# A layer with 32 experts on one core: half of a small projection moved from the middle of the kernel into the first gather, and the low halves of the last token block moved to GpSimd

## The chip, the core and the metric

The kernel runs on one core of a Trainium2 chip. Its engines work side by side and wait for one another by semaphores: TensorE (PE in the profile, PEld for its weight loads) multiplies, VectorE (DVE) and ScalarE (ACT) do elementwise work, GpSimd (POOL) does some of it more slowly, and SyncE (SP) issues all transfers, one after the other, from a queue of its own. The metric is the device time of one execution in microseconds (us); lower is better.

## The reference

One layer over 512 tokens of width 1024, in float32. Cut to what matters here:

```python
x = x + mixed @ w_out                         # attention and recurrence, merged
t = rmsnorm(x, g_moe)
fine = t @ w_rt_expert + b_rt_expert          # routing: top group, then two of its experts
top_logit, top_idx = lax.top_k(fine_sel, 2)
hid = silu(t @ wg) * (t @ wu)                 # 32 experts, 1024 -> 512 -> 1024
acc = acc + c[:, None] * (hid @ wd)
...
gate = sigmoid(rmsnorm(x, g_ple) @ w_ple_gate)
x = x + gate * (p @ w_ple_proj)               # p is 512 x 256, w_ple_proj 256 x 1024
```

p @ w_ple_proj depends on inputs alone. It may be computed anywhere, and is needed only in the last step.

## The kernel before

It works in this order: norm and transposes of x; the recurrent branch; its output projection (`r_stage(0)` to `r_stage(3)`); attention by pairs of heads; its output projection; the product with `w_out` (`out_mm`) with the routing of each block of 128 tokens; the experts, two at a time (`experts(pr)`, 16 pairs); the gate and the final norm.

Accurate products are made of three fast ones: each operand is split into a high part (a copy on ACT into the type fp32r) and a low part (the difference, on VectorE or GpSimd), and high x high, high x low and low x high are added in PSUM (`wsplit` for weights, where a counter hands every third low part to GpSimd).

**p's projection.** `turn_p` transposes and splits p, `p_proj(i)` multiplies it with 512 columns of `w_ple_proj` (24 products for four token blocks), copies the result to SBUF and writes it to the DRAM tile `pp_dram`, which the last stage reads back. `p_proj(0)` stands between `r_stage(1)` and `r_stage(2)`, `p_proj(1)` between `r_stage(2)` and `r_stage(3)`.

**Routing and first gather.** For token block t, `out_route` makes the last logits, `route` picks group and experts (a chain of some 20 small operations on VectorE), ranks the tokens of each expert by products with 0/1 matrices (`rk`), and `one_hot` writes a selection matrix. `split_tokens(t)` makes the high and low half of the block's normed rows (`HX[t]`). `gather_mm` multiplies rows by selection: 16 products for each block, 64 in all, accumulate the tokens of the first four experts (`pt0`, copied to `xg`). For blocks 0 to 2 these stand behind the routing of block 3 in the program; a scheduler may draw them ahead of it. Block 3's follow when its selection is there. Then the first pair's products start: `pair_front`, 16 steps (8 with "g" weights, 8 with "u" weights).

**The ring.** Expert weights come as tiles of 1 MiB, 12 for a pair, 192 in all, into a ring of 15 places (`ra0` to `ra10`, `rb0` to `rb3`) in that order of use, and two more (the first two u tiles of pair 0) into the pool `once`. So 17 tiles can be loaded ahead of the first expert. Every further load waits until the product that reads the tile in its place is done. Four places (`rb0` to `rb3`) hold the merged branches until `out_mm` has read them. Low tiles of memory (`mo`, `once`) share addresses with pools of the earlier stages and come free when those are done. After step 12 of pair 0 the kernel closes `once` and makes the combine weights and their rows (`late_routing`, `in_rows`, on TensorE `row_ps`).

`in_order` fixes TensorE's order for the experts; elsewhere a scheduler orders ready work by priority, and the queues of all engines are fixed before the run. A count `nblk` decides a branch (never taken here) that all engines pass before the experts' main part.

Of the kernel before, what the change touches and what calls it, by code (L numbers as in the profile page):

```python
# [40 lines left out]
def kernel(  # L41
# [20 lines left out]
    def in_order(eng=mybir.EngineType.PE):  # L62
# [6 lines left out]
        for i in ins[start:]:  # L69
            if i.engine == eng:  # L70
# [1 line left out]
                    tc.add_manual_dep(i, prev.name, mybir.DependencyInfo(mybir.DependencyClass.NoSync,  # L72
                                                                         mybir.DependencyReason.DATA), reason="in_order")
                prev = i
    RING_A, RING_B = 11, 4
    W_EARLY = 1
    NRING = RING_A + RING_B
    ONCE = 2

    def SM(name, shape, dt=F32, bufs=4):  # L80
# [459 lines left out]


    pp_dram = dram.tile([S, D], F32, name="pp_dram")

    def turn_p():

        pt = sps("pT_ps")
        for k in range(2):
            for t in range(NT):
                nc.tensor.transpose(pt[:, k, t * P:(t + 1) * P],
                                    pl[t // 2][:, t % 2 * PLE + k * P:t % 2 * PLE + (k + 1) * P], ident)  # L550
            hi, lo = (klp.tile([P, S], F32R, tag=f"kl{n}{k}", bufs=1, name="pt") for n in range(2))
            nc.scalar.activation(hi, pt[:, k, :], AF.Copy)
            nc.vector.tensor_sub(lo, pt[:, k, :], f32(hi))
            PT.append((hi, lo))

    def p_proj(i):
        wh, wl = wsplit(wpp[:, :, i * 512:(i + 1) * 512], [P, 2, 512])
        for t in range(NT):
            ts = slice(t * P, (t + 1) * P)
            if t % 2 == 0:  # L560
                pz2 = sps("pp_ps")
            pz = pz2[:, t % 2, :]
            for k in range(2):
                nc.tensor.matmul(pz, PT[k][0][:, ts], wh[:, k, :], start=k == 0, stop=False)
                nc.tensor.matmul(pz, PT[k][0][:, ts], wl[:, k, :], start=False, stop=False)
                nc.tensor.matmul(pz, PT[k][1][:, ts], wh[:, k, :], start=False, stop=k == 1)
            pe = T("pp")
            nc.scalar.activation(pe, pz, AF.Copy)
            nc.sync.dma_start(pp_dram[ts, i * 512:(i + 1) * 512], pe)

    PT = []
    r_stage(0)
    turn_p()
    r_stage(1)
    wpp = WR([P, 2, D])
    nc.sync.dma_start(wpp, w_ple_proj[0].rearrange("(k p) c -> p k c", p=P))
    p_proj(0)
    r_stage(2)
    p_proj(1)
    r_stage(3)  # L580
    KL = [[klp.tile([P, S], F32R, tag=f"kl{j}{c}", bufs=1, name=f"kl{j}{c}") for c in range(2)] for j in range(2)]
    for j in range(2):
# [85 lines left out]

    G, E = L[:, :, 0:4], L[:, :, 4:36]

    def route(t):

        t0, t1, n, ts_, hs = t, t + 1, 1, (t,), slice(t, t + 1)
        first_max(G, rev4, v4, gmx, f4, t0, t1)
        for t in ts_:
            nc.vector.tensor_scalar(pen[:, t], v4[:, t], f4[:, t:t + 1], NEG, op0=ALU.is_lt, op1=ALU.mult)
        Eh = E[:, hs].rearrange("p t (g e) -> p t g e", g=4)
        nc.vector.tensor_tensor(Eh, Eh, pen[:, hs, :, None].to_broadcast([P, n, 4, 8]), op=ALU.add)
        first_max(E, rev32, v32, m1, f1, t0, t1)
        for t in ts_:  # L680
            nc.vector.tensor_scalar(oh[:, 0, t], v32[:, t], f1[:, t:t + 1], None, op0=ALU.is_equal)
        nc.vector.scalar_tensor_tensor(E[:, hs], oh[:, 0, hs], NEG, E[:, hs], op0=ALU.mult, op1=ALU.add)
        first_max(E, rev32, v32, m2, f2, t0, t1)
        for t in ts_:
            nc.vector.tensor_scalar(oh[:, 1, t], v32[:, t], f2[:, t:t + 1], None, op0=ALU.is_equal)
        rk = tps("rk_ps")[:, 0, 0:32]
        nc.tensor.matmul(rk, ones[0:1, :], e1024b, start=True, stop=False)
        for t2 in range(t):
            for i in range(2):
                nc.tensor.matmul(rk, ones, oh[:, i, t2, :], start=False, stop=False)  # L690
        for i in range(2):
            nc.tensor.matmul(rk, upper, oh[:, i, t, :], start=False, stop=i == 1)
        for i in range(2):
            nc.vector.scalar_tensor_tensor(ohr[:, i, t], oh[:, i, t], 1.0, rk, op0=ALU.mult, op1=ALU.mult,
                                           accum_out=pos[:, i, t:t + 1])

    def split_tokens(t, hx):

        HX[t] = hx
        for i in range(2):  # L700
            cs = slice(i * 512, (i + 1) * 512)
            nc.scalar.activation(hx[:, 0, cs], xm[:, t, cs], AF.Copy, scale=rstd2[:, t:t + 1])
            nc.vector.scalar_tensor_tensor(hx[:, 1, cs], xm[:, t, cs], rstd2[:, t:t + 1], f32(hx[:, 0, cs]),
                                           op0=ALU.mult, op1=ALU.subtract)

# [3 lines left out]
    def one_hot(oneh, pq, t):  # L709
        nc.vector.tensor_scalar(oneh[:, t, :], iota, pq[:, 0, t:t + 1], None, op0=ALU.is_equal)  # L710
        return nc.vector.scalar_tensor_tensor(oneh[:, t, :], iota, pq[:, 1, t:t + 1], f32(oneh[:, t, :]),  # L711
                                       op0=ALU.is_equal, op1=ALU.add)

    def gather_mm(oneh, o, k, ts_):

        for t in ts_:
            for i in range(2):
                c0 = k // 2 * 256 + k % 2
                nc.tensor.matmul(o, HX[t][:, i, c0:c0 + 255:2], oneh[:, t, :],  # L719
                                 start=t == 0 and i == 0 and k % 2 == 0, stop=t == NT - 1 and i == 1 and k % 2 == 1)  # L720

    oneh0 = ONEH()
    pt0 = [sps("xg0_ps").rearrange("p a (k s) -> p (a k) s", k=2) for _ in range(2)]
# [35 lines left out]
        with tc.high_priority():  # L759
            turned[0] = nc.scalar.activation(xTs[j, tt], pt[:, 0:2, :], AF.Copy)  # L760

    def out_route(j, tt):
        for k in range(2):
            kk = 2 * j + k
            nc.tensor.matmul(lg[j, tt], xTs[j, tt][:, k, :], rw[:, kk, :], start=k == 0, stop=k == 1)
        with tc.high_priority():
# [11 lines left out]
        route(tt)  # L778
        hot[0] = one_hot(oneh0, pos, tt)
    wo = {}  # L780
    prev = None
    for j, tt in [(j, t) for j in range(2) for t in range(NT)] + [(j, t) for t in range(NT) for j in (2, 3)]:
        if j not in wo:
            raw = wraw(w_out[0], 256 * j)
            wo[j] = wo_block(raw, 0, False) + wo_block(raw, 1, 3 == j)
        pz = zps("out_ps")[:, 0:256]
        out_mm(pz, wo[j], tt, range(2))
        if prev:
            out_turn(*prev)
        out_mm(pz, wo[j], tt, range(2, KT))  # L790
        if prev:
            out_route(*prev)
        out_add(j, tt, pz)
        prev = j, tt
    with tc.high_priority():
        out_turn(*prev)
        out_route(*prev)
    for k in range(KT):
        gather_mm(oneh0, pt0[k // 4][:, k % 4, :], k, range(3))


    mx_stack.close()
# [4 lines left out]
    ring = [(ring_a, f"ra{i}") for i in range(RING_A)] + [(ring_b, f"rb{i}") for i in range(RING_B)]  # L807

    def RING(name, dt=F32):

# [4 lines left out]
    W = {}  # L815

    def gate_load(b):
        W["ple", b] = WR([P, 2, D]) if b < 3 else mo.tile([P, 2, D], F32, tag="hx3", bufs=1, name="wgr")
        nc.sync.dma_start(W["ple", b], w_ple_gate[0, 256 * b:256 * b + 256, :].rearrange("(k p) c -> p k c", p=P))

    def pair_order():
# [5 lines left out]
                yield pr - 1, "d", w_e_down  # L827
        yield NE // 2 - 1, "d", w_e_down

    def loads():  # L830
        for pr, nm, src in pair_order():
            if pr == 15 and nm == "d":
                for b in range(W_EARLY):
                    gate_load(b)
            for h in range(4):
                n = P if nm == "d" else 2 * P
                if (pr, nm) == (0, "u") and h < ONCE:
                    t = once.tile([P, 2, D], F32, name=f"once{h}")
                else:
                    t = RING(nm)  # L840
                s_ = src[0, 2 * pr:2 * pr + 2, h * n:(h + 1) * n, :]
                s_ = s_.rearrange("e (p k) f -> p e (k f)", k=2)
# [3 lines left out]
                nc.sync.dma_start(*W[pr, nm, h])  # L846
                yield

    loader = loads()
# [9 lines left out]
        used[0] += n  # L859
        load_upto(used[0] + (ONCE if used[0] < 8 else 0) + len(ring))  # L860

    load_upto(NRING + ONCE - 0)

    late = []

    def MT(name, shape=(P, 512), dt=F32):
        return late[0].tile(list(shape), dt, tag="mt", bufs=6, name=name)

    split_tokens(3, mo.tile([P, 2, D], F32R, tag="hx3", bufs=1, name="hx3"))
    posb = mo.tile([P, 2, S], F32, name="posb")  # L870
    wb = mo.tile([P, 2, S], F32, name="wb")
    pcol = mo.tile([P, NE // 2], F32, name="pcol")
# [247 lines left out]
    def front_fill(pr):  # L1120
        def fill(step, last):
# [3 lines left out]
                scatter_two(pr - 2, 0)  # L1125
            if step == SLOTS_AT and pr:
                slots_of(pr - 1)
            if pr == 0 and step == 12:
                once_stack.close()
                late.append(ctx.enter_context(tc.tile_pool(name="late", bufs=1)))  # L1130
                with tc.issue_after(last.ins):
                    late_routing()
                    in_rows(pos, posb)
                    in_rows(wts, wb)
# [172 lines left out]
```

## Time and profile before

| | |
|---|---|
| time, median of 3 runs | 1128.45 us (1127.37 to 1129.65) |
| the profiled execution | 1131.39 us, its span 1129.7 us |
| TensorE busy | 1096.9 us, 97% of the span |
| VectorE, ScalarE, GpSimd busy | 568.0, 382.6, 156.1 us |
| mean granted TensorE clock | 0.987 of full speed |

A row of the timeline gives the start, the length, the engine, the line of the kernel, what is written and read, the shape, a count, and in brackets how long the engine sat idle before it and for whom. Products follow each other faster than the length of one, since they are pipelined: the distance of their starts is their cost. Line numbers are those of the kernel before. Names drop their buffer numbers: `wr` is a weight buffer or, in the gather, a block's rows, `hx` the rows of block 3.

### The profile page before, as it was taken

The page shows a single profiled execution, that of the slowest core. Times are in us where ns is not written, and L with a number is a line of the kernel's source. Part 1 is how long each engine was busy: PE and PEld are TensorE (multiplying, and loading weights), DVE is VectorE, ACT ScalarE, POOL GpSimd, SP SyncE. Part 2 cuts the span into 40 slices and gives each one's busy share as a digit, 9 for nine tenths or more (in the row PEclk, how much of TensorE's full clock was granted, in tenths as well). Part 3 has the DMA queues.
Part 4 walks back from the last instruction along what each step waited for, and adds up shares of the span by engine and source line. Part 5 has one row for each costly group of instructions (what it writes and reads, how often), then busy time and mean ns, then how long its engine had stood idle before and what let it go on. Part 6 is the DMA issues. An engine that isn't in the chain of part 4 may idle for free. (4 is left out here: it accounts for less than half of the span.)

```text
span 1129.7 us, 14413 instructions
## 1 busy us (share of the span) xinstructions
PE 1096.9 (97%) x5650; PEld 740.1 (66%) x5650; DVE 568.0 (50%) x1080; ACT 382.6 (34%) x771; POOL 156.1 (14%) x142
## 2 busy tenths in 40 slices
PE   8999999999999999999989999999999999999897
PEld 7777777788787878778984535353545353533376
DVE  5766675236566574664474334334333334233653
ACT  5455544335455454634322202020202011111443
POOL 4242423111122121233100000000000000000201
PEclk8999999999999999999999999999999999999899
DMA  7322231522222212136748999999999999999601
GB/s 207 112 87 82 74 132 60 184 84 72 72 75 75 76 62 75 52 108 233 270 176 307 396 413 413 412 414 413 412 412 411 412 413 414 413 413 416 270 20 56
DMA packets 101602, 259.81 MB, mean 230 GB/s; under 512 B 12477, under 2 KB 56090, under 8 KB 93338
## 3 DMA queue, kind: packets, MB, share of 16 engines
q1 hardware_dynamic: 101530, 258.84, 60.2%
q8 instruction: 46, 0.75, 0.3%
q14 instruction: 26, 0.21, 0.1%
HBM read 254.63 MB, written 4.19 MB: 229 GB/s over the span
## 5 line engine op out<-in xcount | busy, mean ns | idle before, releaser
L1032 PE MATMUL y_ps<-d,hT 128*64 128x512 f32 x512 | 118.3, 602 | 2.2 <-DMA d<-in_w_e_down_dram 2.2
L158 ACT ACTIVATE wh<-wr 128x1024 fp32r<-128x1024 f32 x81 | 85.5, 1057 | 98.1 <-PE R_ps L171 21.9
L1018 PE MATMUL gu_ps<-g,xg 128*64 128x512 f32 x512 | 116.8, 595 | 0.1
L1018 PE MATMUL gu_ps<-u,xg 128*64 128x512 f32 x496 | 110.1, 592 | 0.0
L161 DVE TENSOR_TENSOR wl<-wr,wh 128x1024 fp32r<-128x1024 f32 x54 | 73.0, 1352 | 60.3 <-ACT wh L158 58.9
L161 POOL TENSOR_TENSOR wl<-wr,wh 128x1024 fp32r<-128x1024 f32 x27 | 66.0, 2444 | 175.3 <-ACT wh L158 161.9
L1023 ACT ACTIVATE sg<-gu_ps 128x512 f32<-128x512 f32 x16 | 9.6, 598 | 235.5 <-PE gu_ps L1018 235.5
L1032 PEld LDWEIGHTS y_ps<-d,hT 128*64 128x64 f32 x512 | 36.2, 138 | 73.2 <-issue 67.2
L1018 PEld LDWEIGHTS gu_ps<-g,xg 128*64 128x64 f32 x512 | 37.1, 137 | 69.1 <-issue 64.4
L1018 PEld LDWEIGHTS gu_ps<-u,xg 128*64 128x64 f32 x496 | 35.8, 137 | 70.3 <-issue 69.0
L1024 DVE TENSOR_TENSOR sg<-sg,gu_ps 128x512 f32<-128x512 f32 x16 | 11.0, 687 | 120.8 <-ACT sg L1023 120.8
L1223 POOL TENSOR_TENSOR wgl<-wr,wgh 128x1024 fp32r<-128x1024 f32 x2 | 4.7, 2380 | 481.1 <-DMA PP<-pp_dram 481.1
L994 DVE TENSOR_TENSOR xm<-xm,comb_ps 128x1024 f32<-128x1024 f32 x30 | 36.6, 1221 | 60.5 <-PE comb_ps L993 60.5
L719 PE MATMUL xg_ps<-oneh,wr 128*128 128x256 f32 x384 | 58.2, 290 | 2.1 <-DVE oneh L711 2.1
L976 DVE SCALAR_TENSOR_TENSOR yl<-y_ps,c,yh 128x512 fp32r<-128x512 f32 x30 | 22.5, 750 | 73.4 <-ACT yh L975 71.5
L975 ACT ACTIVATE yh<-y_ps,c 128x512 fp32r<-128x512 f32 x30 | 20.6, 688 | 100.6 <-PE y_ps L1032 100.6
L719 PEld LDWEIGHTS xg_ps<-oneh,wr 128*128 128x128 f32 x384 | 52.7, 201 | 2.8 <-DVE oneh L711 2.2
L172 PE MATMUL merge_ps<-hTh,wl 128*128 128x512 f32 x128 | 51.8, 405 | 0.0
L170 PE MATMUL merge_ps<-hTh,wh 128*128 128x512 f32 x128 | 51.4, 402 | 0.0
L171 PE MATMUL merge_ps<-hTl,wh 128*128 128x512 f32 x128 | 51.4, 401 | 0.0
L985 DVE TENSOR_TENSOR xm<-xm,comb_ps 128x512 f32<-128x512 f32 x68 | 43.8, 680 | 4.7 <-PE comb_ps L983 4.4
L944 ACT ACTIVATE xg<-xg_ps,gm 128x256 f32<-128x256 f32 x60 | 25.2, 471 | 53.6 <-PE xg_ps L719 53.5
(329 smaller groups left out, 2526.4 us busy)
## 6 DMA issues: line engine op xcount, KB each, us to landing
g<-in_w_e_gate_dram SPq DMA_DIRECT2D x64, 1024.0 KB, 18.9
d<-in_w_e_down_dram SPq DMA_DIRECT2D x64, 1024.0 KB, 19.9
u<-in_w_e_up_dram SPq DMA_DIRECT2D x62, 1024.0 KB, 18.7
wr<-in_w_in_dram SPq DMA_DIRECT2D x26, 1024.0 KB, 5.1
wr<-in_w_lru_br_dram SPq DMA_DIRECT2D x4, 1024.0 KB
wr<-in_w_attn_br_dram SPq DMA_DIRECT2D x4, 1024.0 KB, 5.2
wr<-in_w_out_dram SPq DMA_DIRECT2D x4, 1024.0 KB, 5.2
wr<-in_w_ple_gate_dram SPq DMA_DIRECT2D x3, 1024.0 KB
```

The lines of the kernel that those rows point to most:

```text
L158: nc.scalar.activation(hi, src, AF.Copy)
L161: e.tensor_sub(lo, src, f32(hi))
L170: nc.tensor.matmul(out_ps, wh[:, k, :], th(k), start=k == 0, stop=False)
L171: nc.tensor.matmul(out_ps, wh[:, k, :], tl(k), start=False, stop=False)
L172: last = nc.tensor.matmul(out_ps, wl[:, k, :], th(k), start=False, stop=k == KT - 1)
L719: nc.tensor.matmul(o, HX[t][:, i, c0:c0 + 255:2], oneh[:, t, :], start=t == 0 and i == 0 and k % 2 == 0, stop=t == NT - 1 and i == 1 and k ...
L944: xg_out["a"] = nc.scalar.activation(xg[(k + c) // 2][:, (k + c) % 2, :], pt[:, c, :], AF.Copy, scale=gm2[:, k + c:k + c + 1])
L976: nc.vector.scalar_tensor_tensor(yl, y, c[:, 0:1], f32(yh), op0=ALU.mult, op1=ALU.subtract)
L985: nc.vector.tensor_tensor(xs_, xs_, pc, op=ALU.add)
L994: nc.vector.tensor_tensor(xm[:, t, :], xm[:, t, :], pc.rearrange("p a b -> p (a b)"), op=ALU.add)
L1018: last = nc.tensor.matmul(gu[i][64 * e:64 * e + 64, :], xg[k // 2][:, k % 2, o + 64 * e:o + 64 * e + 64], W[pr, nm, k // 2][0][:, e, k % 2 ...
L1032: nc.tensor.matmul(py[i][64 * e:64 * e + 64, :], hT[:, f, 64 * e:64 * e + 64], W[pr, "d", f // 2 * 2 + e][0][:, f % 2, i * 512:(i + 1) * 5 ...
```

## The change

The second half of p's projection leaves its place between `r_stage(2)` and `r_stage(3)`. `turn_p` now also writes the transposed p to DRAM (`pt_dram`); before the last part of `out_mm` is built, `p_split` reads it and the second half of `w_ple_proj` back in four loads of 256 KB and splits them on ACT and VectorE. The 24 products (`p_late(0)` to `p_late(3)`, six for each token block) stand in the first gather, in an order written out by hand. Block 3's low halves are made on GpSimd, from an extra copy on ACT; its rows get a place of the ring's memory (`hx3`), and the ring's fifteenth place moves to `mo` (`rc`). The tiles in `once` are now the last two u tiles of pair 0, and they are issued behind all others. `once` is closed after step 15.

```diff
-    RING_A, RING_B = 11, 4
+    RING_A, RING_B = 10, 4
-    NRING = RING_A + RING_B
+    NRING = RING_A + RING_B + 1
...
 def turn_p():
+            raw = T("praw")
+            nc.scalar.activation(raw, pt[:, k, :], AF.Copy)
+            nc.sync.dma_start(pt_dram[k], raw)
...
     r_stage(2)
-    p_proj(1)
     r_stage(3)
...
 def split_tokens(t, hx):
             nc.scalar.activation(hx[:, 0, cs], xm[:, t, cs], AF.Copy, scale=rstd2[:, t:t + 1])
+            if t == 3:
+                xn = PE("xn")
+                nc.scalar.activation(xn, xm[:, t, cs], AF.Copy, scale=rstd2[:, t:t + 1])
+                nc.gpsimd.tensor_sub(hx[:, 1, cs], xn, f32(hx[:, 0, cs]))
+                continue
...
+    def p_late(t):
+        pz = zps("pp2_ps")
+        p_mm(pz, t, lambda k: wp2[k][0], lambda k: wp2[k][1])
+        p_keep(pz, t, 1, PE("pe"))
+    PE = lambda name: mr.tile([P, S], F32, tag="pe", bufs=3, name=name)
+    def p_split():
+        for (hi, lo), src in zip(wp2 + PT, (wpp2[:, 0, 512:1024], wpp2[:, 1, 512:1024], pt_dram[0], pt_dram[1])):
+            raw = PE("p2raw")
+            nc.sync.dma_start(raw, src)
+            nc.scalar.activation(hi, raw, AF.Copy)
+            nc.vector.tensor_sub(lo, raw, f32(hi))
...
-    with tc.high_priority():
-        out_turn(*prev)
-        out_route(*prev)
-    for k in range(KT):
-        gather_mm(oneh0, pt0[k // 4][:, k % 4, :], k, range(3))
+    def fill():
+        p_late(0)
+        gather0(2)
+    with in_order():
+        gather0(0)
+        with tc.high_priority():
+            out_turn(*prev)
+        gather0(1)
+        with tc.high_priority():
+            out_route(*prev, fill, lambda: p_late(1))
+        p_late(2)
+        p_late(3)
...
-                if (pr, nm) == (0, "u") and h < ONCE:
+                if (pr, nm) == (0, "u") and h >= 4 - ONCE:
...
-    load_upto(NRING + ONCE - 0)
+    load_upto(NRING + ONCE)
+    for z in later:
+        nc.sync.dma_start(*z)
-    split_tokens(3, mo.tile([P, 2, D], F32R, tag="hx3", bufs=1, name="hx3"))
...
-            if pr == 0 and step == 12:
+            if pr == 0 and step == 15:
```

TensorE's queue at the end of the first gather, before: the last products of blocks 0 to 2 (`xg_ps<-oneh,wr`) stand between the rank and count products (`rk_ps`, `cnt_ps`), then block 3's 16, then three steps of the first pair, and the branch.

```order
L719 MATMUL xg_ps<-oneh,wr 128x256 x8
L884 LDWEIGHTS ones
L884 MATMUL cnt_ps<-oh,ones 128x32
L692 LDWEIGHTS upper
L692 MATMUL rk_ps<-oh,upper 128x32
L719 MATMUL xg_ps<-oneh,wr 128x256 x8
L719 MATMUL xg_ps<-oneh,hx_5231 128x256 x16
L1018 MATMUL gu_ps<-g,xg 64x512 x3
```

After, from the second half of block 0's gather on (`xmT_ps<-ident,xm` is the last transpose before the logits `xmT_ps<-rw,xmT` of block 3; `pp_ps<-p` are p's products):

```order
L742 MATMUL xg_ps<-oneh,wr 128x256 x9
L792 MATMUL xmT_ps<-ident,xm 128x128 x2
L742 MATMUL xg_ps<-oneh,wr 128x256 x16
L800 MATMUL xmT_ps<-rw,xmT 128x36 x2
L563 MATMUL pp_ps<-p_4368,p_4372 128x512
L564 MATMUL pp_ps<-p_4369,p_4372 128x512
L565 MATMUL pp_ps<-p_4368,p_4373 128x512
L563 MATMUL pp_ps<-p_4370,p_4374 128x512
L564 MATMUL pp_ps<-p_4371,p_4374 128x512
L565 MATMUL pp_ps<-p_4370,p_4375 128x512
L742 MATMUL xg_ps<-oneh,wr 128x256 x16
L563 MATMUL pp_ps<-p_4368,p_4372 128x512
```

Six products of p now stand ahead of block 2's gather and six behind it, ahead of the rank products; twelve more stand between the rank products and block 3's gather. The transpose and the logits of block 3 each stand behind a whole block's gather.

SyncE's queue ahead of the branch, before (g, u, d are ring loads):

```order
L846 DMA g<-in_w_e_gate_dram 128x2x1024 x4
L846 DMA u<-in_w_e_up_dram 128x2x1024 x4
L846 DMA d<-in_w_e_down_dram 128x2048
L846 DMA once_5205<-in_w_e_up_dram 128x2x1024
L846 DMA once_5207<-in_w_e_up_dram 128x2x1024
L1158 TENSOR_LOAD nblk_i
L1158 ISA x2
L1159 COMPARE_AND_BRANCH
```

And after:

```order
L900 DMA u<-in_w_e_up_dram 128x2x1024 x4
L569 DMA pp_dram<-pe 128x512 x3
L900 DMA d<-in_w_e_down_dram 128x2048
L569 DMA pp_dram<-pe 128x512
L1213 TENSOR_LOAD nblk_i
L1213 ISA x2
L900 DMA d<-in_w_e_down_dram 128x2048
L918 DMA once_5247<-in_w_e_up_dram 128x2x1024
L918 DMA once_5248<-in_w_e_up_dram 128x2x1024
L900 DMA d<-in_w_e_down_dram 128x2048
L1214 COMPARE_AND_BRANCH
```

The first d load (into `rc`) now stands behind three of the four writes of p's results. The second d load, which waits until the first expert's products have read a g tile, stands ahead of the two `once` loads, which before were issued ahead of all experts.

## Rows read from the trace of the kernel before

**Rows 1.** The page: its first line.

```profile
span 1129.7 us, 14413 instructions
```

**Rows 2.** Windows: stretch, length; PE, PEld, DVE, ACT, POOL busy; clock; DMA share; GB/s.

```profile
222.70:577.80 355.10, 351.38 (x2084) 298.43 (x2082) 204.17 (x483) 162.69 (x410) 74.18 (x65) 1.00 0.32 108
580.00:585.00 5.00, 2.86 (x21) 2.67 (x21) 3.86 (x13) 1.34 (x2) 0.85 (x1) 0.75 1.00 374
588.00:595.00 7.00, 6.55 (x42) 4.63 (x42) 3.77 (x20) 2.25 (x5) 0.00 (x0) 1.00 0.03 8
600.00:1047.00 447.00, 444.60 (x2228) 208.70 (x2223) 166.47 (x262) 67.55 (x124) 0.00 (x0) 1.00 1.01 409
635.00:640.00 5.00, 5.00 (x26) 1.68 (x24) 0.97 (x2) 1.38 (x2) 0.00 (x0) 1.00 0.88 315
```

**Rows 3.** The chain that ended last, from 990 us on: start, length, what.

```profile
1023.97 20.55 DMA d<-in_w_e_down_dram
...
1044.58 19.46 DMA PP<-pp_dram
```

**Rows 4.** Timeline of PE at the second half of p's projection.

```profile
216.12 0.39 PE L564 MATMUL pp_ps<-wh,pt 128*128 128x512 f32 x1
...
220.31 0.40 PE L170 MATMUL R_ps<-yh,wh 128*128 128x512 f32 x1
```

**Rows 5.** Timeline of PE in the first gather and the first pair.

```profile
577.65 0.53 PE L765 MATMUL xmT_ps<-rw,xmT 128*128 128x36 f32 x4
578.01 0.98 PE L719 MATMUL xg_ps<-oneh,wr 128*128 128x256 f32 x6
578.83 0.38 PE L757 MATMUL xmT_ps<-ident,xm 128*128 128x128 f32 x2
...
582.85 2.29 PE L719 MATMUL xg_ps<-oneh,wr 128*128 128x256 f32 x9 [2.14 <-DVE oneh L711]
584.94 0.39 PE L884 MATMUL cnt_ps<-oh,ones 128*128 128x32 bf16 x6
585.16 2.39 PE L719 MATMUL xg_ps<-oneh,wr 128*128 128x256 f32 x15
...
590.09 2.16 PE L719 MATMUL xg_ps<-oneh,hx 128*128 128x256 f32 x16 [0.30 <-DVE cmax L889]
592.18 7.84 PE L1018 MATMUL gu_ps<-g,xg 128*64 128x512 f32 x31
...
604.68 1.09 PE L909 MATMUL row_ps<-ident,pos 128*128 128x128 f32 x8
```

**Rows 6.** The chain that ended last: a later gather of four experts.

```profile
624.29 7.68 PE xg_ps L719 x64
```

**Rows 7.** Timeline of DVE in the routing of block 3.

```profile
581.64 0.75 DVE L703 SCALAR_TENSOR_TENSOR hx<-xm,rstd,hx 128x512 fp32r<-128x512 f32 x1 [0.94 <-ACT hx L702]
...
583.54 0.25 DVE L655 SCALAR_TENSOR_TENSOR L<-xmT_ps,rstd,L 128x36 f32<-128x36 f32 x1
...
586.91 0.24 DVE L685 TENSOR_SCALAR oh<-v,f 128x32 bf16<-128x32 f32 x1
```

**Rows 8.** Timeline of DVE, and of POOL, 486 to 496 us.

```profile
489.41 0.88 DVE L619 TENSOR_TENSOR mx<-mg,mx 128x128 fp32r<-128x128 f32 x4
492.63 2.73 DVE L619 TENSOR_TENSOR mx<-mg,mx 128x128 fp32r<-128x128 f32 x4 [1.74 <-ACT mx L618]
492.21 2.40 POOL L161 TENSOR_TENSOR wl<-wr,wh 128x1024 fp32r<-128x1024 f32 x1
```

**Rows 9.** Timeline of ACT behind the routing of block 3.

```profile
592.30 1.80 ACT L944 ACTIVATE xg<-xg_ps,gm 128x256 f32<-128x256 f32 x4 [10.08 <-PE xg_ps L719]
```

**Rows 10.** Timeline of SP's DMA issues around the first pair.

```profile
580.71 0.88 SPq L846 DMA_DIRECT2D once<-in_w_e_up_dram  x2
595.34 0.36 SPq L846 DMA_DIRECT2D d<-in_w_e_down_dram  x1
...
635.58 0.33 SPq L846 DMA_DIRECT2D d<-in_w_e_down_dram  x1
```

More of the change, by code (lines that the diff above doesn't have):

```diff
@@ L542 @@
     pp_dram = dram.tile([S, D], F32, name="pp_dram")
+    pt_dram = dram.tile([2, P, S], F32, name="pt_dram")
     def turn_p():
@@ L554, in turn_p, with p_mm, p_keep @@
             PT.append((hi, lo))
+            raw = T("praw")
+            nc.scalar.activation(raw, pt[:, k, :], AF.Copy)
+            nc.sync.dma_start(pt_dram[k], raw)
+    def p_mm(pz, t, wh, wl):
+        ts = slice(t * P, (t + 1) * P)
+        for k in range(2):
+            nc.tensor.matmul(pz, PT[k][0][:, ts], wh(k), start=k == 0, stop=False)
+            nc.tensor.matmul(pz, PT[k][0][:, ts], wl(k), start=False, stop=False)
+            nc.tensor.matmul(pz, PT[k][1][:, ts], wh(k), start=False, stop=k == 1)
+    def p_keep(pz, t, i, pe):
+        nc.scalar.activation(pe, pz, AF.Copy)
+        nc.sync.dma_start(pp_dram[t * P:(t + 1) * P, i * 512:(i + 1) * 512], pe)
     def p_proj(i):
-        wh, wl = wsplit(wpp[:, :, i * 512:(i + 1) * 512], [P, 2, 512])
+        wh, wl = wsplit(wpp, [P, 2, 512])
         for t in range(NT):
-            ts = slice(t * P, (t + 1) * P)
             if t % 2 == 0:
                 pz2 = sps("pp_ps")
[L562 to L569, printed above, removed]
+            p_mm(pz2[:, t % 2, :], t, lambda k: wh[:, k, :], lambda k: wl[:, k, :])
+            p_keep(pz2[:, t % 2, :], t, i, T("pp"))
     PT = []
@@ L574 @@
     r_stage(1)
-    wpp = WR([P, 2, D])
-    nc.sync.dma_start(wpp, w_ple_proj[0].rearrange("(k p) c -> p k c", p=P))
+    wpp2 = w_ple_proj[0].rearrange("(k p) c -> p k c", p=P)
+    wpp = WR([P, 2, 512])
+    nc.sync.dma_start(wpp, wpp2[:, :, 0:512])
     p_proj(0)
     r_stage(2)
-    p_proj(1)
     r_stage(3)
@@ L669, with route @@
     G, E = L[:, :, 0:4], L[:, :, 4:36]
-    def route(t):
+    def route(t, between=lambda: None):
         t0, t1, n, ts_, hs = t, t + 1, 1, (t,), slice(t, t + 1)
@@ L685, in route @@
             nc.vector.tensor_scalar(oh[:, 1, t], v32[:, t], f2[:, t:t + 1], None, op0=ALU.is_equal)
+        between()
         rk = tps("rk_ps")[:, 0, 0:32]
@@ L712, in one_hot, with gather0 @@
                                        op0=ALU.is_equal, op1=ALU.add)
+    def gather0(t):
+        for k in range(KT):
+            gather_mm(oneh0, pt0[k // 4][:, k % 4, :], k, (t,))
+    def p_late(t):
+        pz = zps("pp2_ps")
+        p_mm(pz, t, lambda k: wp2[k][0], lambda k: wp2[k][1])
+        p_keep(pz, t, 1, PE("pe"))
     def gather_mm(oneh, o, k, ts_):
@@ L720, in gather_mm @@
                                  start=t == 0 and i == 0 and k % 2 == 0, stop=t == NT - 1 and i == 1 and k % 2 == 1)
+    GT = lambda name: merge.tile([P, S], F32R, tag="gate", bufs=8, name=name)
+    wp2, PT = ([[GT("p2") for n in range(2)] for k in range(2)] for _ in range(2))
+    PE = lambda name: mr.tile([P, S], F32, tag="pe", bufs=3, name=name)
[5 more added lines that the diff above has]
+            nc.vector.tensor_sub(lo, raw, f32(hi))
     oneh0 = ONEH()
@@ L760, in out_turn, with out_route @@
             turned[0] = nc.scalar.activation(xTs[j, tt], pt[:, 0:2, :], AF.Copy)
-    def out_route(j, tt):
+    def out_route(j, tt, fill=lambda: None, between=lambda: None):
         for k in range(2):
@@ L765, in out_route @@
             nc.tensor.matmul(lg[j, tt], xTs[j, tt][:, k, :], rw[:, kk, :], start=k == 0, stop=k == 1)
+        fill()
         with tc.high_priority():
@@ L777, in out_route @@
                 split_tokens(tt, WR([P, 2, D], F32R))
-        route(tt)
+        else:
+            with tc.high_priority(), tc.issue_after(turned[0].ins):
+                split_tokens(tt, ring_a.tile([P, 2, D], F32R, tag="hx3", bufs=1, name="hx3"))
+        route(tt, between)
         hot[0] = one_hot(oneh0, pos, tt)
@@ L782 @@
     for j, tt in [(j, t) for j in range(2) for t in range(NT)] + [(j, t) for t in range(NT) for j in (2, 3)]:
+        if (j, tt) == (2, 0):
+            p_split()
         if j not in wo:
@@ L806 @@
     once = once_stack.enter_context(tc.tile_pool(name="once", bufs=1))
-    ring = [(ring_a, f"ra{i}") for i in range(RING_A)] + [(ring_b, f"rb{i}") for i in range(RING_B)]
+    ring = [(ring_a, f"ra{i}") for i in range(RING_A)] + [(ring_b, f"rb{i}") for i in range(RING_B)] + [(mo, "rc")]
     def RING(name, dt=F32):
@@ L817, in gate_load @@
     def gate_load(b):
-        W["ple", b] = WR([P, 2, D]) if b < 3 else mo.tile([P, 2, D], F32, tag="hx3", bufs=1, name="wgr")
+        W["ple", b] = WR([P, 2, D]) if b < 3 else ring_a.tile([P, 2, D], F32, tag="hx3", bufs=1, name="wgr")
         nc.sync.dma_start(W["ple", b], w_ple_gate[0, 256 * b:256 * b + 256, :].rearrange("(k p) c -> p k c", p=P))
@@ L828, in pair_order @@
         yield NE // 2 - 1, "d", w_e_down
+    later = []
     def loads():
@@ L845, in loads @@
                 W[pr, nm, h] = t, s_
-                nc.sync.dma_start(*W[pr, nm, h])
+                if (pr, nm) == (0, "u") and h >= 4 - ONCE:
+                    later.append((t, s_))
+                else:
+                    nc.sync.dma_start(*W[pr, nm, h])
                 yield
```

## The prediction

> **What bounds the kernel now.** I read the windows of the trace first, then the chain that ended last, then the timeline of the first gather, engine by engine. Over the 355 us ahead of the gather TensorE works for 351.38 of 355.10 us, at the full clock [rows 2]: it is the bound, and what leaves its queue there is gained nearly whole. From 600 to 1047 us both TensorE (444.60 of 447) and the transfers (409 GB/s, a share of 1.01) are full [rows 2], and the chain of waits ends in transfers alone, 20.55 us of a weight load and 19.46 us of PP [rows 3]: there the bytes set the end. 409 GB/s is 2.56 us for a tile of 1 MiB.
>
> Between the two lies the gather, 578.01 to 592.18 us, 14.17 us in which TensorE is not the bound. It idles 2.14 us for VectorE's selection `oneh`, and the window 580 to 585 has 2.86 busy us of 5 at a granted clock of 0.75, so part of it at 1.2 GHz [rows 2, 5]. On VectorE the logits of block 3 end at 583.54 and both one-hot tiles `oh` at 587.15 (586.91 + 0.24), a routing of 3.6 us; in front of it VectorE waits 0.94 us for ACT's `hx` and spends 0.75 us on a low half [rows 7].
>
> Does an earlier start of the experts move the end, if bytes set it? The stream is fed by places of the ring. From 588 to 595 us nothing more can be loaded and 8 GB/s flow [rows 2]; the first load into a freed place is issued at 595.34, 3.2 us after the first expert's first product (592.18) [rows 5, 10]. Transfers that idle for want of a free place start earlier when the experts do, so the end follows the experts' start. That is the step on which everything hangs.
>
> **The removal.** The second half's first product starts at 216.12, the first of `r_stage(3)` at 220.31, and 18 of the 24 products stand between: 4.19 / 18 = 0.233 us each [rows 4]. 24 of them are 5.6 us of a full TensorE. The split, four copies and four writes that go too lie beside it. In exchange this stretch gets four copies on ACT and four differences on VectorE (`p_split`), two copies more in `turn_p`, and 1.5 MiB of transfers where their share is 0.32 [rows 2]; ACT is busy 162.69 and VectorE 204.17 us of 355, so I put them at nothing. If they, or the changed turn of `wsplit`'s counter, delay an operand, the price is idle time of TensorE; all of it in that stretch is now 3.72 us. I take a bound of half of this, 1.7 to 1.9, either way: **-5.6, between -7.3 and -3.9**.
>
> **The gather.** TensorE's work there, after, from the place of 578.01 on: 64 products at 0.120, their price in a later gather at the full clock [rows 6], are 7.7; p's 24 are 5.6; the transposes and logits of block 3 at most 0.38 + 0.53, with the overlap of queued products 0.6; some 18 small rank and count products at 0.037 (six take the 0.22 between 584.94 and 585.16 [rows 5]) 0.7. Sum 14.6, against 14.17 now: **+0.4**. The clock should stay at 1.00, since the idle time ahead of its fall is filled. At best the small ones and logits hide beside others (-0.9 against now), at worst they cost 1.2.
>
> That holds if nothing on VectorE comes later than TensorE reaches it. The order of after puts two blocks' gathers (2 x 1.9) and the transposes ahead of the logits, which then end near 582.5; behind them stand p's six and block 2's gather and six more of p (1.4 + 1.9 + 1.4), so the rank products are reached near 587.3. VectorE must have `oh` by then. It no longer makes low halves (two of 0.75) nor waits 0.94 for them [rows 7], so its routing of 3.6 us may start at once behind the logits and end near 586.5: 0.8 us in hand. The second chain, from the rank products (587.43) to block 3's first product (590.09), is 2.7 us [rows 5] and lies beside `p_late(2)` and `p_late(3)`, 2.8 us. ACT is idle for 10.08 us there now [rows 9], and can make four copies of p's results and the two extra ones.
>
> GpSimd's differences are what can eat these margins. No such operation runs in the gather now. The nearest is a `wl` of 128x1024 at 2.40 us, so 1.2 us for each of two halves of 512. Beside it the same four `mx` products on VectorE took 2.73 instead of 0.88 us [rows 8]. If one or both meet the routing they hold it for up to 1.2 us each, of which 0.8 is in hand: 0 to +1.4, and I take **+0.6**, since at least one of the two should be done before the logits end.
>
> The Trainium skill, SBUF — State Buffer, section "SBUF: two separate sides", says that VectorE (with two inputs from SBUF) and GpSimd share a port pair as an exclusive lock, held for a whole instruction. The pair of rows agrees; by this rule the cost would come in whole operations of GpSimd, the upper bound just given, and a total of 0.8 us more than I forecast.
>
> So the experts start 5.6 - 1.0 = 4.6 us earlier: at 587.6.
>
> **The loads.** SyncE's queue, after, has the first d load behind three writes of p's results (the third `p_late` ends near 590 in times of before) and the second d load, which waits for a freed place, ahead of the two `once` loads. Before, all three were transferred ahead of the experts (`once` issued at 580.71 [rows 10]). So 7.7 us of transfers move behind, partly into 588 to 595, which is empty now. Behind it there is room too: from the first freed place (595.34) to the fifteenth (635.58) there are 40.2 us for 14 tiles of 2.56, 35.8, and the window 635 to 640 shows the queue run dry (share 0.88) [rows 2, 10]. Room is 4.4 us, and the first d uses the empty stretch; what two `once` tiles (5.1) exceed it by is 0.7. If the d tile finds no room either, 3.3 less what bursts hide: 0 to +2.9, I take **+0.6**.
>
> **Sum:** -5.6 + 0.4 + 0.6 + 0.6 = -4.0. The profiled execution took 1131.39 us (span 1129.7 [rows 1]), 2.9 above the median; with the same difference its median of 1128.45 becomes **1124.4 us**.
>
> **The rivals.** *No measurable change* (within 0.2%, 2.3 us, about what a measurement of this kernel can tell). Two mechanisms lead there. In one, both of GpSimd's differences fall into the routing (+1.4) and the d tile comes too late (+2.9): -5.6 + 0.4 + 1.4 + 2.9 = -0.9, 1127.6. In the other the bytes set the end wherever the experts start, 1128 to 1128.5; for it speaks the share of 1.01 over 447 us, against it the seven empty microseconds ahead of it and the dry queue at 635 [rows 2]. Chance 0.18 together.
>
> *Slower.* The `once` tiles are now those that steps 12 to 15 of pair 0 read. Step 12 stands at 604.68, and a step is (604.68 - 592.18) / 12 = 1.04 us [rows 5]. In times of before, shifted by the gather's +1.0, the second d load issues at 596.3; three tiles behind it take 7.7 us, so the first `once` is through at 601.4 and the second at 604.0, needed at 605.7 and 607.8. How long a load takes to land beyond its bytes no row here shows; 4 us are in hand. Each microsecond beyond stops TensorE, and with it the freeing of places, while the transfers have nothing to catch up with. It decides against the change from 4.0 + 2.3 = 6.3 us of stop, a landing 10 us after its bytes are due. That needs the second d load to be held as well: it waits in SyncE's queue behind the last write of p's results and the load of `nblk`. At 7 us of stop: 1131.5. Against it: the queue's order makes the wait one, not a sum, since both earlier entries are done before the first expert runs. Chance 0.14.
>
> **How the numbers follow.** The forecast, faster by over 0.2%, has 0.68; the rivals 0.18 and 0.14. The low end takes the removal at its best with no hold of VectorE and no loss in the loads: -7.3 + 0.4 = -6.9, 1121.5. The high end takes the removal at its worst with all other bounds: -3.9 + 0.4 + 1.4 + 2.9 = +0.8, 1129.2, which takes in the case of no change. Below lies some 0.05, above the slower case.
>
> **What would show it.** Right: no product of p's second half near 216 us and no new idle time ahead of the gather; `gu_ps` starting near 587.6; no wait of 2 us for `oneh`, and a clock of 1.00 in the gather; `once` landed before step 12; the fifteenth freed place's load near 631; the weight stream's end 4 us earlier. Wrong: idle time of TensorE ahead of the rank products or block 3's gather (GpSimd or a late `oh`), ahead of step 12 (`once`), or an end of the stream that stays although the experts start earlier.

## The result and the profile after

The changed kernel takes 1135.38 us (median of 6 runs, 1133.4 to 1136.31) against 1128.34 us for the kernel before (6 runs, 1124.36 to 1133.62): a ratio of 1.0067, 95% interval 1.0048 to 1.0085. It is slower, by some 7.5 us, where 1124.4 was forecast. The profiled execution took 1136.31 us, against 1131.39 for that of before.

The gather came out near its forecast: 15.77 us from the logits of block 2 to the first pair, 14.53 before, so +1.24 where +1.0 was forecast. TensorE's timeline of the changed kernel, from the logits of block 2 to the first pair (that of before is [rows 5]):

```profile
571.38 0.53 PE L800 MATMUL xmT_ps<-rw,xmT 128*128 128x36 f32 x4
571.75 1.09 PE L742 MATMUL xg_ps<-oneh,wr 128*128 128x256 f32 x7
...
576.06 0.53 PE L800 MATMUL xmT_ps<-rw,xmT 128*128 128x36 f32 x4
...
582.08 0.18 PE L939 MATMUL cnt_ps<-oh,ones 128*128 128x32 bf16 x1 [0.31 <-DVE oh L693]
...
585.14 2.08 PE L742 MATMUL xg_ps<-oneh,hx 128*128 128x256 f32 x16
587.15 7.09 PE L1073 MATMUL gu_ps<-g,xg 128*64 128x512 f32 x32
603.96 5.82 PE L1073 MATMUL gu_ps<-u,xg 128*64 128x512 f32 x16 [9.72 <-SPq L1214]
609.60 2.75 PE L1073 MATMUL gu_ps<-once,xg 128*64 128x512 f32 x12
```

The wait of 2.14 us for `oneh` is gone, and the experts start at 587.15 (forecast 587.6). That the two agree is luck: this execution is 2.1 us ahead of the other already at the first `R_ps` product (169.5 against 171.6, rows of experiment 8). From there to the experts it is 417.65 us, against 420.58 before, so 2.9 us are gained where 4.6 were forecast. Then, all 32 g products done, TensorE stands still for 9.72 us ahead of its first u product. The load of that tile was issued at 518 us. What released the product is line 1214 on SyncE's queue: the branch. And the 16 products after the pause take 5.82 us, where 16 took 3.65 in a kernel below that doesn't pause.

Windows of the changed kernel (start and end, length; busy us of PE, PEld, DVE, ACT, POOL; clock; DMA share; GB/s), of the gather, of the g products, of the pause in two parts, and behind it:

```profile
571.00:587.00 16.00, 15.69 (x121) 14.26 (x119) 11.20 (x44) 6.99 (x13) 3.87 (x6) 1.00 0.37 122
...
587.20:594.20 7.00, 7.00 (x33) 2.15 (x32) 4.74 (x22) 3.27 (x7) 0.00 (x0) 1.00 0.94 344
594.20:601.40 7.20, 0.03 (x2) 0.00 (x0) 0.00 (x0) 0.00 (x0) 0.00 (x0) 0.77 1.01 408
601.40:603.90 2.50, 0.00 (x0) 0.00 (x0) 0.00 (x0) 0.00 (x0) 0.00 (x0) 0.50 0.10 43
603.90:609.60 5.70, 5.64 (x17) 1.90 (x19) 0.00 (x0) 0.00 (x0) 0.00 (x0) 0.61 0.77 280
```

No engine works in the pause. Its first 7.2 us are full of transfers (408 GB/s); TensorE moves some 2.5 us after these have run out (43 GB/s). The granted clock has fallen to 0.50 by then and is 0.61 over the next 5.7 us, so 1.2 GHz for most of that stretch.

The chain that ended last of the changed kernel (that of before is [rows 3]):

```profile
1031.31 20.07 DMA d<-in_w_e_down_dram
1051.44 17.92 DMA PP<-pp_dram
```

It still ends in transfers, and its last one starts at 1051.44 where it started at 1044.58, in an execution that was 2.1 us ahead early on: what the pause kept the ring from loading was not made up.

SyncE's DMA issues of the changed kernel around the pause:

```profile
585.38 0.33 SPq L900 DMA_DIRECT2D d<-in_w_e_down_dram  x1
585.96 0.32 SPq L569 DMA_DIRECT2D pp_dram<-pe  x1
589.12 0.34 SPq L900 DMA_DIRECT2D d<-in_w_e_down_dram  x1
592.06 0.90 SPq L918 DMA_DIRECT2D once<-in_w_e_up_dram  x2
593.01 11.57 SPq L900 DMA_DIRECT2D d<-in_w_e_down_dram  x2
604.69 14.52 SPq L900 DMA_DIRECT2D g<-in_w_e_gate_dram  x4
```

SyncE's waits at the branch in the changed kernel (who waited for whom: total, times, longest):

```profile
SPq L1214 <- SPq L1214: 10.2, 3, 5.3
```

In the kernel before, the same row of the branch, which my prediction did not look at:

```profile
SPq L1159 <- SPq L1159: 2.7, 1, 2.7
```

Between 589.12 and 593.01 SyncE issues four loads of 1 MiB (a d tile, both `once` tiles, a d tile); then nothing leaves its queue for some 11 us. What it stands at is written in the program. SyncE's rows around the branch in the changed kernel, with the semaphores that each waits for (the DMAHW ones count finished transfers), and TensorE's first product behind it:

```
100 L900 DMA d<-in_w_e_down_dram 128x2048 [waits DMAHW7_49,PE_49]
101 L918 DMA once_5247<-in_w_e_up_dram 128x2x1024 [waits DMAHW3_49,DMAHW4_49,DMAHW2_49,DMAHW6_49,DMAHW0_49,Pool_49]
102 L918 DMA once_5248<-in_w_e_up_dram 128x2x1024 [waits DMAHW1_49]
103 L900 DMA d<-in_w_e_down_dram 128x2048 [waits PE_49]
104 L1214 COMPARE_AND_BRANCH
...
171 L1214 UNCONDITIONAL_BRANCH [waits DMAHW0_49,DMAHW1_49,DMAHW2_49,DMAHW3_49,DMAHW4_49,DMAHW5_49,DMAHW6_49,DMAHW7_49]
172 L900 DMA d<-in_w_e_down_dram 128x2048 [waits DMAHW3_49,PE_49]

2919 L1214 UNCONDITIONAL_BRANCH [waits PE_49]
2920 L1073 MATMUL gu_ps<-u,xg 64x512 [waits DMAHW3_49,DMAHW0_49,DVE_49]
```

Behind the body SyncE has a row, on the path that skips it, that waits on all eight counters of transfers before it goes on: on everything it has issued (in experiment 1, whose body has no transfers, no such row is left). The body of the branch reloads the four u tiles of pair 0 behind its own use of them, so TensorE's first u product waits on a counter that the skipped body would have raised. SyncE raises it in its place once it has drained. In the program each of the eight waits is for all that was issued on its counter ahead of the branch and is followed by an addition of what the body would have added; `DMAHW3_49` is waited for at 208 and raised by 64, and TensorE's first u product waits for it at 272. The three counters of the `once` tiles and the last d tile stand ahead of it in that row. The program before has the same wait, but both `once` loads were issued at 580.71 [rows 10] and the next load stands behind the branch, so the queue was empty there (8 GB/s from 588 us on [rows 2]).

### The profile page after: what moved, and what is told of

Same layout as the page of the kernel before. It is cut to its first block, busy times and chain, and to the rows that moved or that the text cites. A ratio compares the mean times of both kernels' runs of the same rounds, so it can differ in the third digit from the quotient of the medians.

```text
span 1134.6 us, 14446 instructions
## 1 busy us (share of the span) xinstructions
PE 1093.7 (96%) x5650; PEld 734.6 (65%) x5650; DVE 574.3 (51%) x1082; ACT 386.9 (34%) x778; POOL 155.0 (14%) x143
## 5 line engine op out<-in xcount | busy, mean ns | idle before, releaser
L161 POOL TENSOR_TENSOR wl<-wr,wh 128x1024 fp32r<-128x1024 f32 x26 | 63.1, 2428 | 160.2 <-ACT wh L158 147.7
```

The costliest lines, as they stand in the source:

```text
L161: e.tensor_sub(lo, src, f32(hi))
```

## The experiments

Three theories were set against each other. *Drain*: the above. *Code*: the branch is the price itself, because the code behind it has to be loaded while weights fill the queues. *Late tiles*: the forecast's own slower rival, the `once` tiles land too late for step 12.

**1. No transfers in the branch.**

```diff
-                        nc.sync.dma_start(w, src[0, ds(e, 1), k * P:(k + 1) * P, :].rearrange("o p f -> p (o f)"))
+                        nc.gpsimd.memset(w, 0.0)
...
-                        nc.sync.dma_start(w, w_e_down[0, ds(e, 1), f * P:(f + 1) * P, cs].rearrange("o p f -> p (o f)"))
+                        nc.gpsimd.memset(w, 0.0)
...
-        for h in range(4):
-            nc.sync.dma_start(*W[0, "u", h])
```

> The changed kernel with the same queues up to the branch, but the transfers inside the branch that is never taken are left out (weights of the overflow are zeros there, and the four u tiles are not reloaded). Drain theory: in the changed kernel SyncE stands at the branch until all its loads have landed (near 603 us), and TensorE's first u product waits for that, 9.7 us; without transfers in the body nothing has to be waited for, so this idle time is gone. What may be left is a wait of 0 to 2 us for the once tiles at step 12. Time 1123 to 1127 us. Rival, code: the branch is still there and the code behind it has to be loaded while weights fill the queues: TensorE idles some 10 us at the same place, 1135 us. Rival, late tiles: the idle time moves to step 12 and is some 5 us, 1130 us.

1123.21 us (10 runs), ratio 0.998, interval 0.9962 to 0.9998. Its first u and first `once` products on TensorE:

```profile
594.12 3.65 PE L1073 MATMUL gu_ps<-u,xg 128*64 128x512 f32 x16 [1.81 <-PEq L1212]
597.57 3.63 PE L1073 MATMUL gu_ps<-once,xg 128*64 128x512 f32 x16
```

Same queues, same branch, never taken in either kernel, and 9.72 us became 1.81, put down to TensorE's own sequencer at the branch. What is left stands there, and not at step 12, where I had it. The code theory is out as the main cause; the late tiles too, since no product of `once` waits.

**2. The waiting d loads behind the branch.** Each load that the loader issues behind the branch in the program is held behind it in SyncE's queue as well:

```diff
+    def behind_branch(i):
+        if branch[0] is not None:
+            tc.add_manual_dep(i, branch[0].name, mybir.DependencyInfo(mybir.DependencyClass.NoSync,
+                                                                      mybir.DependencyReason.DATA), reason="behind_branch")
...
             loaded[0] += 1
+            if loaded[0] <= 24:
+                behind_branch(nc.cur_bb.bb.instructions[-1])
...
         overflow(nb)
+    branch[0] = nc.cur_bb.bb.instructions[-1]
```

> The changed kernel with the d loads of pair 0 that wait for freed places put behind the branch in SyncE's queue; the two once loads stay ahead of it. Drain theory: SyncE waits for the two once tiles alone, issued near 592 and landed near 598 to 599, so TensorE idles 4 to 5 us ahead of its first u product in place of 9.7, 1129 to 1131 us. Rival, code: two of four tiles are still queued ahead of the code, some 5 to 7 us. Rival, late tiles: no idle time ahead of the first u product, 0 to 1 us at step 12, 1125 us.

1129.68 us, ratio 1.0026 (1.0011 to 1.0041).

```profile
601.18 5.28 PE L1082 MATMUL gu_ps<-u,xg 128*64 128x512 f32 x16 [6.75 <-SPq L1223]
```

Two loads ahead of the branch in place of four, and 6.75 us in place of 9.72. That is 3.0 us less where two tiles fewer are 5.1 us of traffic. `once` is issued at 591.83 here too, since it waits until the last write of p's results has landed, and until then the transfers run half empty: 203 GB/s between 587.2 and 594.2 us, against 344 in the changed kernel. My 4 to 5 us had left that out, and the time from the last bytes to TensorE's product, some 2.5 us. By itself the 6.75 lies in the range that I had given the code rival (5 to 7); what speaks against that rival is experiments 1 and 5.

**3. All of them behind the branch, `once` first** (with `behind_branch` of experiment 2).

```diff
-    for z in later:
-        nc.sync.dma_start(*z)
...
+    branch[0] = nc.cur_bb.bb.instructions[-1]
+    for z in later:
+        nc.sync.dma_start(*z)
+        behind_branch(nc.cur_bb.bb.instructions[-1])
```

> The changed kernel with the once loads and the d loads that wait for freed places all behind the branch in SyncE's queue, once first. Drain theory: only the first d tile and the last write of p's results have to land, near 592, before TensorE is through with the g products at 594.2: no idle time ahead of the first u product; the once tiles land near 597 to 599 and may cost 0 to 1.5 us at steps 12 and 14. 1123 to 1126 us, faster than the kernel before by 0.2 to 0.5%. Rival, late tiles: once is issued no earlier than in the changed kernel, so some 4 us are lost at step 12, 1128 us or more.

1126.65 us, ratio 0.9992 (0.9972 to 1.0013): no difference to the kernel before can be told.

```profile
592.25 3.88 PE L1079 MATMUL gu_ps<-u,xg 128*64 128x512 f32 x15
597.08 1.94 PE L1079 MATMUL gu_ps<-once,xg 128*64 128x512 f32 x8 [0.95 <-DMA once<-in_w_e_up_dram]
599.63 1.94 PE L1079 MATMUL gu_ps<-once,xg 128*64 128x512 f32 x8 [0.62 <-DMA once<-in_w_e_up_dram]
```

The pause at the branch is gone, as the drain theory has it; the late tiles are real, at 1.6 us, not the 6.3 that would have decided. The total, 1126.65, missed my 1123 to 1126 by a little.

**4. No branch.**

```diff
-    with tc.issue_after(xg_out["a"].ins), tc.issue_after(xg_out["v"].ins):
-        nb = nc.values_load(nblk_i[0:1, 0:1], min_val=0, max_val=4)
-    with tc.If(nb > 0):
-        overflow(nb)
```

> The changed kernel without the branch and its body (the overflow, which this input never needs, is left out). Drain theory and code theory: no idle time ahead of the first u product; the order of the loads is that of the changed kernel (d, once, once, d), so the once tiles land near 599 to 601 and cost 1 to 3 us at step 12. 1124 to 1127 us. Rival, late tiles: 5 us or more at step 12, 1130 us.

1125.07 us, ratio 0.9988 (0.997 to 1.0007): inside the forecast, and no difference to the kernel before can be told. TensorE does not stop ahead of u, and `once` costs 0.32 + 0.61 us at the same two steps as in experiment 3:

```profile
599.96 1.94 PE L1073 MATMUL gu_ps<-once,xg 128*64 128x512 f32 x8 [0.32 <-DMA once<-in_w_e_up_dram]
602.50 1.94 PE L1073 MATMUL gu_ps<-once,xg 128*64 128x512 f32 x8 [0.61 <-DMA once<-in_w_e_up_dram]
```

**5. The overflow's transfers issued by GpSimd.** The computation is whole:

```diff
-                        nc.sync.dma_start(w, src[0, ds(e, 1),
+                        nc.gpsimd.dma_start(w, src[0, ds(e, 1),
...
-                        nc.sync.dma_start(w, w_e_down[0, ds(e, 1),
+                        nc.gpsimd.dma_start(w, w_e_down[0, ds(e, 1),
...
-            nc.sync.dma_start(*W[0, "u", h])
+            nc.gpsimd.dma_start(*W[0, "u", h])
```

> The changed kernel, whole, with the transfers inside the branch issued by GpSimd in place of SyncE (24 lines of the body, never executed for this input). Drain theory: SyncE has nothing of its own to wait for at the branch, so the time is that of the kernel without those transfers: no more than 2 us of idle time ahead of the first u product, 1122.5 to 1125 us, ratio 0.996 to 0.999 to the kernel before. Rival: the drain moves to GpSimd, which has no transfer of its own under way then, so it would cost nothing either; if the branch itself and its code are the price, 6 to 10 us stay, 1130 us or more.

1123.86 us (12 runs), against 1127.83 for the kernel before beside it: ratio 0.9968 (0.9952 to 0.9984), faster than both kernels.

```profile
568.93 0.53 PE L800 MATMUL xmT_ps<-rw,xmT 128*128 128x36 f32 x4
...
584.70 7.09 PE L1073 MATMUL gu_ps<-g,xg 128*64 128x512 f32 x32
593.63 3.65 PE L1073 MATMUL gu_ps<-u,xg 128*64 128x512 f32 x16 [1.85 <-PEq L1214]
597.09 3.79 PE L1073 MATMUL gu_ps<-once,xg 128*64 128x512 f32 x16
...
603.46 1.14 PE L964 MATMUL row_ps<-ident,wts 128*128 128x128 f32 x8 [1.56 <-ACT posb L965]
```

SyncE has no wait at the branch any more. The d, `once`, `once`, d order of its queue is that of the changed kernel, so the order alone was no fault: only the order ahead of a drain.

**6. Block 3's low halves on VectorE again** (on top of experiment 5).

```diff
-            if t == 3:
-                xn = PE("xn")
-                nc.scalar.activation(xn, xm[:, t, cs], AF.Copy, scale=rstd2[:, t:t + 1])
-                nc.gpsimd.tensor_sub(hx[:, 1, cs], xn, f32(hx[:, 0, cs]))
-                continue
```

> The same with one part of the change undone: block 3's low halves by VectorE again (two differences of 0.75 us, straight from the rows), not by GpSimd. If GpSimd's differences hold VectorE's routing (my term of 0.6 us), the gather is shorter by up to 0.6 us here less the 1.5 us of VectorE that come back, so 0 to 1.5 us longer: TensorE idles 0.5 to 1.5 us more ahead of the rank products. Rival, that they cost nothing and save VectorE 1.5 us ahead of its chain: 0.8 to 1.5 us longer. Rival, that the halves lie beside TensorE's work in any case: the same gather to 0.3 us. The total within 1.5 us of the run above.

1124.27 us, ratio 0.9969 (0.9952 to 0.9985), not to be told from experiment 5. The gather can be read in the traces. VectorE in the changed kernel, two kinds of operation of the routing, each first alone and then beside GpSimd's differences:

```profile
578.33 0.25 DVE L674 SCALAR_TENSOR_TENSOR v<-L,m,rev 128x32 f32<-128x32 f32 x1
...
578.84 0.24 DVE L689 TENSOR_SCALAR oh<-v,f 128x32 bf16<-128x32 f32 x1
...
579.57 1.23 DVE L674 SCALAR_TENSOR_TENSOR v<-L,m,rev 128x32 f32<-128x32 f32 x1
...
581.05 0.98 DVE L693 TENSOR_SCALAR oh<-v,f 128x32 bf16<-128x32 f32 x1
```

GpSimd in the changed kernel, the two differences:

```profile
579.45 2.54 POOL L715 TENSOR_TENSOR hx<-xn,hx 128x512 fp32r<-128x512 f32 x2 [4.87 <-ACT xn L714]
```

VectorE in experiment 6, the later two of these operations, with GpSimd idle:

```profile
578.18 0.25 DVE L674 SCALAR_TENSOR_TENSOR v<-L,m,rev 128x32 f32<-128x32 f32 x1
...
578.69 0.24 DVE L693 TENSOR_SCALAR oh<-v,f 128x32 bf16<-128x32 f32 x1
```

TensorE in experiment 6, the two ends of the gather:

```profile
569.98 0.53 PE L795 MATMUL xmT_ps<-rw,xmT 128*128 128x36 f32 x4
...
585.29 7.09 PE L1068 MATMUL gu_ps<-g,xg 128*64 128x512 f32 x32
```

GpSimd's work lengthens the routing by 0.98 + 0.74 = 1.7 us, of which most was in hand: from the logits of block 2 to the experts it is 584.70 - 568.93 = 15.77 us with GpSimd (experiment 5; 15.74 to 15.77 in the changed kernel and experiments 1 to 3, 16.10 in 4) and 585.29 - 569.98 = 15.31 without, a cost of 0.46 (the prediction's term: 0.6). VectorE's two halves that come back cost nothing: they fit into its wait for the logits. So the hold is real, but the expectation missed: the gather is 0.46 us shorter here, where I had 0 to 1.5 longer, and no wait of TensorE for `oh` is left. The rival that GpSimd saves 0.8 to 1.5 us is refuted; the same gather to 0.3 us is missed too, by little. The Trainium skill, SBUF — State Buffer, section "SBUF: two separate sides", has VectorE and GpSimd exclude each other for a whole instruction; the trace agrees in kind and size (one operation of VectorE held by 0.98 us, one by 0.74, by two of GpSimd that last 2.54 together).

**7. The move undone, the rest kept** (p's second half at its old place; new ring, late `once`, written order, GpSimd's halves and the branch stay).

```diff
     p_proj(0)
     r_stage(2)
+    p_proj(1)
...
-        p_late(0)
         gather0(2)
...
-            out_route(*prev, fill, lambda: p_late(1))
-        p_late(2)
-        p_late(3)
+            out_route(*prev, fill)
```

> The changed kernel with p's second half at its old place (between the second and third r_stage), so without the four products in the gather, their writes and the four loads; the new ring, the late once tiles, the written order of the gather, GpSimd's halves and the branch as in the changed kernel. Without the four writes ahead of it, SyncE issues once before the first expert; what stays behind them ahead of the branch is one d load. Drain theory: TensorE idles ahead of the first product behind the branch only until that one d tile has landed: 0 to 3 us. Experts start as before (590 to 592.5), total 1126 to 1131 us. If the late once tiles or the new ring are at fault by themselves, without the writes: 6 us or more of idle time, 1133 us.

1126.55 us, ratio 0.9994 (0.9977 to 1.0011). Without the writes, `once` is issued at 582.03, and only one d load waits ahead of the branch:

```profile
598.20 3.65 PE L1067 MATMUL gu_ps<-u,xg 128*64 128x512 f32 x16 [0.22 <-issue]
```

SyncE still stands 5.6 us at the branch, for that one tile, but is through by the time TensorE has done its g products. So the pause needs the moved part too: the writes of p's results, which hold `once` until after the first expert has begun.

**8. The kernel before without the second half.**

```diff
-            nc.sync.dma_start(pp_dram[ts, i * 512:(i + 1) * 512], pe)
+            for half in range(2):
+                nc.sync.dma_start(pp_dram[ts, half * 512:(half + 1) * 512], pe)
...
-    p_proj(1)
```

> The kernel before with the second half of p's product left out (its split and 24 products; the first half's results are written in its place, so the writes stay). This prices the removal alone, with everything behind it as it was. If the end follows the experts' start, as the prediction took it: -5.6 us, 1120 to 1122 us, ratio 0.995. If the bytes of the weight stream set the end wherever the experts start: no change, ratio 0.999 to 1.001. If the idle time that the changed kernel has between 224 and 571 us (2 us more than before) comes with the removal itself, -3.6 to -4.

1121.3 us (6 runs), ratio 0.9942 (0.992 to 0.9965), some 6.5 us. The end follows the experts' start, and the rival that the bytes set the end wherever the experts start is refuted. The third, -3.6 to -4, lies at the edge of the interval (-9.0 to -3.9). Among the products of the recurrent branch's projection stand those of p. Their group in the kernel before (count, ns of one: least, mean, most; first to last):

```profile
L170 PE MATMUL R_ps<-yh,wh x64: 392/396/632, 171.6 to 232.2; 128*128 128x512 f32 x64
```

In the changed kernel:

```profile
L170 PE MATMUL R_ps<-yh,wh x64: 392/396/628, 169.5 to 224.5; 128*128 128x512 f32 x64
```

And in this one:

```profile
L170 PE MATMUL R_ps<-yh,wh x64: 392/396/505, 169.6 to 223.1; 128*128 128x512 f32 x64
```

## Why the prediction was wrong, step by step

**Bounds: right.** TensorE's queue ahead of the gather is worth its time, and the end follows the experts' start (experiment 8).

**The removal, -5.6 between -7.3 and -3.9: right.** The stretch of the three rows is 60.6 us before and 55.0 after, 5.6 less. It is known to some 1.5 us only: with the same products in it the stretch takes 55.0 us in experiments 2 and 4 and 53.4 to 53.5 in 1, 3, 5, 6 and 8. From its end to the logits of block 2 it is 577.65 - 232.2 = 345.45 us before [rows 5] and 571.38 - 224.5 = 346.9 after, so 1.4 us are given back, inside my bound of 1.7 to 1.9. Some 1.0 of them come with the removal alone (the same two places in experiment 8: 569.58 - 223.1 = 346.5), and none is left with the move undone (in experiment 7: 574.81 - 229.3 = 345.5). Net -4.2, where my sum went on with -5.6 and took the bound for the worst case alone.

**The gather, +1.0: right.** From the logits of block 2 to the experts 14.53 us before and 15.77 after, +1.24, with 0.46 of it GpSimd's. TensorE idles 0.31 us in it, for `oh`, one of the signs named. The clock is 1.00 there. Two sizes in it were off and nearly cancel: both differences met the routing, for 1.7 us, where I had hoped for one at most (1.2); and the slack ahead of the rank products is 1.2 us by the prediction's own numbers (582.5 + 3.6 is 586.1, not 586.5), not 0.8. In experiment 6, without the hold, `oh` is there at 578.93 and TensorE comes to it near 580.1.

**The loads, +0.6 between 0 and 2.9: this is the step that failed.** "SyncE's queue, after, has the first d load behind three writes of p's results and the second d load, which waits for a freed place, ahead of the two `once` loads" was the right observation, priced as bytes that move into an empty stretch, at +0.6; it came to some 10 us. That the branch stands behind these loads, and that SyncE does not pass it before every one of them has landed, was in no term, and a stop there is not among the signs of being wrong. The slower rival had the queue and its writes, but put the stop at step 12 and waited for tiles; it stands at step 8, in front of a tile that is there, and waits for the counters. The late tiles themselves cost 0 to 1.6 us (experiments 1, 3 to 5). The argument I set against that rival, that both earlier entries are done before the first expert runs, also failed: the last write was issued at 585.96 and `once` waited 2.4 us more for it to land, to 592.06. So the slower outcome, given 0.14, came by a mechanism that nothing in the prediction had.

**The size of it.** The pause is 9.72 - 1.85 = 7.9 us longer than in experiment 5, and the 16 products behind it take 5.82 - 3.65 = 2.2 us longer at the lower clock: 10.1 us. The ratios of the two kernels, 1.0067 and 0.9968, differ by 0.0099, 11.2 us, so the pause accounts for nearly all of it. With the pause out of the way the kernel is at -3.6 (ratio 0.9968, -5.4 to -1.8), and my sum was -4.0. That does not bear out its terms one by one: the experts start 2.9 us earlier, not 4.6, and TensorE still stops 1.85 us at the branch and 1.56 us for `posb`, which the sum left out. `posb` belongs to the rows of the combine weights, which stand behind step 15 now and not behind step 12; in the kernel before the wait is 0.25 us:

```profile
606.01 1.14 PE L909 MATMUL row_ps<-ident,wts 128*128 128x128 f32 x8 [0.25 <-ACT posb L910]
```

How these add up to -3.6 is not shown; single executions of one kernel lie some 6 us apart (1121.02 to 1127.31 in experiment 5).

## What to carry to other kernels

A branch that is never taken can still be a place at which a queue stops: look, for each engine, at what the skipped path waits for, and at what stands ahead of it in the queue, before moving a load across it. A load that waits for a freed place ties everything behind it to the work that frees the place; ahead of a drain it ties TensorE to itself. When a program waits on counters, "the tile has landed" doesn't mean that its reader may start; the cure here was to issue the body's transfers from a queue that has nothing else under way.

## What the runs showed of the hardware that was not expected

- At the branch TensorE starts some 2.5 us after the transfers end: in the changed kernel the traffic falls off near 601.4 and the first product comes at 603.96.
- Passing the branch costs TensorE 1.81, 1.85 and 2.10 us where weights fill the queues (experiments 1, 5 and 6), put down to its own sequencer; 0.22 us in experiment 7, where 4 GB/s flow from 596 to 598 us; nothing that shows in the kernel before, which passes it at 8 GB/s [rows 2]; and nothing where there is no branch (experiment 4). That fits code behind the branch that comes in late beside the weights, but it was not tried.
- The granted clock is 0.50 at the end of the pause and 0.61 over the 5.7 us behind it, so 1.2 GHz for most of them.
- `oh`, an operation with one tensor input (0.24 us alone), was held to 0.98 us beside GpSimd, like the one with two.
- Executions differ before anything changed can act: the first R_ps product starts at 171.6 us in the trace of before and 169.5 in that of after, 2.1 us apart, so times of single traces are compared here from a common place on.
